# Attention's values as two block products of three factors in half the rows, with forms and buffers kept across layers

## The chip, the cores and the metric

The kernel runs on one core of a Trainium2 chip. The metric is the device time of one execution in microseconds (us). Matrix products run on TensorE (PE in the profile; its weight loads are PEld), elementwise work on VectorE (DVE) and ScalarE (ACT); GpSimd (POOL) and SyncE (SP) here only start DMAs. Each engine works through its own instructions in order.

## The reference

A decoder trunk of two layers for 256 tokens of width 2048 in float32. Layer 0 has a recurrent mixer, layer 1 dilated sliding-window attention with 16 heads of 128; each is followed by an MLP with squared ReLU (2048 to 8192 and back). What matters here is the start of layer 1:

```python
hn = rms_norm(h, norm_mix[layer])
qkv = (hn @ w_qkv).astype(F32).reshape(bsz, seq, 3, ATTN_HEADS, HEAD_DIM)
q = partial_rope(qkv[:, :, 0], positions) * (HEAD_DIM ** -0.5)
k = partial_rope(qkv[:, :, 1], positions)
v = qkv[:, :, 2]
...
out = (num / den).reshape(bsz, seq, D_MODEL).astype(h.dtype)   # softmax(q k) v, three masks merged
return out @ w_o
```

## The kernel before

**Numbers in two parts.** Float32 matrices go through TensorE as a high and a low part, and a product is high x high + high x low + low x high, three matmuls. Activations lie in `bufa` or `bufb` with both parts. Weights come from memory in units of 128 x 2048 (1 MB), and are split by `Weights.split` (lines 99 to 103): ACT copies the high part (L102), DVE subtracts to get the low part (L103). There are three buffers each for raw, high and low units. All units of the kernel stand in one list, `units`, in the order of use; `unit()` (L170) hands out the next one and starts the load and the split of the one two places further on.

**Order.** A list scheduler puts each engine's instructions in order by priority as they become ready; the loads and splits of weights have a raised priority (`stream`, offset 150), the emptying of accumulators a higher one (`urgent`, offset 400). All large matmuls are chained in program order by `mm` (L180). `turn` puts transposes into that chain, and `later`/`flush` hold back the work of `to_features` and `to_h` until a unit's matmuls are out.

**A pass of blocks() (L648).** In the MLP, two column groups of 512 are made in one pass. The 16 row blocks of the weights are in two halves. Eight plain row blocks are multiplied as usual: four units marked `n`, each for two halves of the tokens (j = 0, 1), 24 matmuls a unit. The other eight are taken in four pairs, and with two token halves and two column groups they form 2 x 2 by 2 x 2 block products, which take seven products for eight (units `a`, `t1`, `t2`, `c`, `t3`, `d`, `t4`; 12 matmuls each). The right-hand sides of four of them are sums of weight units: `s` = a + t1, then s + c (DVE, L130), `t1` with c's partner added by an accumulating DMA on POOL (L142), and for w1 a last one by such a DMA too (L148). Their left-hand sides are sums of activation blocks, the *forms*: `formx` for `bufa`, made by `to_features` (L614) with `combos` and `part_forms`, and `formh` for `bufb`. A pass makes 180 matmuls of 512 columns and 11 splits. It uses four accumulator banks: `alpha`, `delta`, `gamma` from the pool `pmm` and `beta`, named `po` or `pd`. Banks are reused within a pass, and callers give `events`, which empty a bank behind a product.

**The end of layer 0.** `mlp(0, ...)` makes four quarters of two w1 passes (`first`) and two w2 passes (`second`, adding to the residual `xres` by L751). In the last quarter each finished column group n is squared and summed for the next norm (L291), then transposed, scaled and split into `bufa` by `to_features(n, "nmix1")`, without forms (L235, L236). The groups come out in the order 1, 0, 3, 2.

**Attention.** `rstd(nx1)` makes the norm's factor `rt` (a column per token half; L295, L296, L317 to L322 on DVE); `over_tokens` transposes it into the bank `pt` (L307), ACT copies it to `rs` (L845). `tokens_group` makes four heads' values: 4 units of 24 matmuls into two banks, emptied at the end by ACT with factor `rt` (L348). `scores(u0)` projects a head's q and k (16 matmuls of 512 and 16 of 256 columns each), scales them by `rs`, turns them (`rope`, with tables made once by `rotary`, L814), and makes softmax and its transpose `pT`; `mix` multiplies by the values into `bufb`. The order is values 0, heads 0 to 3, values 1, heads 4 to 7, values 2, heads 8 to 11, the scores of heads 12 to 15, values 3, their mixes. Then `out_project` multiplies by w_o, four units of 24 matmuls for each column group, the unit of heads 12 to 15 last.

Of the kernel before, what the change touches and what calls it, by code (L numbers as in the profile page):

```python
# [41 lines left out]
def trunk_kernel(ctx, tc, x, xtok, cols, tab, masks, pos, fin, w_in, w_gate, w_out, w_qkv, w_o, w1, w2, out):  # L42
# [81 lines left out]
    def combine(u, src, i, what, i0):  # L124
        def load(name, j, home=wraw):
            held[name] = home.tile([P, 2048], F32, name="raw" if home is wraw else name)
            nc.sync.dma_start(held[name], src[j])

        def add(to, x, y):
            V.tensor_tensor(held[to], held[x], held[y], OP.add)  # L130

        if what == "a":
            load("t1", i0 + 4, pair)
            load("a", i)
            held["s"] = pair.tile([P, 2048], F32, name="s")
            add("s", "a", "t1")
        elif what in ("n", "d"):
            load(what, i)
        ahead = units[u + 1][2:3] if u + 1 < len(units) else ()
        if ahead == ("t2",):  # L140
            load("c", i0 + 5)
            nc.gpsimd.dma_start(held["t1"], src[i0 + 5], accum_op=OP.add)  # L142
            add("s", "s", "c")
        if ahead == ("t4",) and src not in T4_DMA(w1, w2):
            add("s", "s", "d")
        made[u] = Weights(held[{"t1": "s", "t2": "s", "t3": "t1", "t4": "s"}.get(what, what)])
        if what == "c" and src in T4_DMA(w1, w2):
            nc.gpsimd.dma_start(held["s"], src[i0 + 1], accum_op=OP.add)  # L148
# [175 lines left out]
    def tokens(src, i0, mov, kgs=(0, 1, 2, 3), by_k=False):  # L324
        ks = PAIRED if src is w2 else range(KB)
        ps = [pmm.tile([P, 512], F32, name="p") for _ in range(2)]
# [260 lines left out]
    def open_pairs(layer):  # L587
        pool_ = pairs.enter_context(tc.tile_pool(name=f"pair{layer}", bufs=1))
        return pool_, [pool_.tile([P, 4, 2, 512], F32R, name=n) for n in ("formx", "formh")]

# [10 lines left out]

    pair, (formx, formh) = open_pairs(0)

# [44 lines left out]
    def blocks(src, i0, n0, mov, forms, events, final):  # L648
# [20 lines left out]
        plains = [0, 0]  # L669
        for what, u in ORDERS[src is w2]:  # L670
            w = unit(src, None if u is None else i0 + 4 * n0 + u)
            if what != "n":
                times(bank[what], w, side[what])
                if what in events:
                    events[what](bank[what])
                continue
            n, g = divmod(u, 4)
            plains[n] += 1
            due = len(later)
            for j in (1, 0) if n else (0, 1):  # L680
                times(sums[n, j], w, lambda i, j=j, g=g: plain(j, 4 * g + i))
                if plains[n] == 2:
                    final(n, j, sums[n, j])
            flush(due)
# [85 lines left out]
    def mlp(layer, nrm, nxt, gname):  # L770
# [8 lines left out]
        r2 = nrm.inv_mean()  # L779
        r2n = tmp.tile([P, 2], F32, name="r2n", bufs=2)  # L780
# [26 lines left out]

    vgs = mixers.enter_context(tc.tile_pool(name="vgs1", bufs=2))
    wk = mixers.enter_context(tc.tile_pool(name="wk2", bufs=2))
    rot = mixers.enter_context(tc.tile_pool(name="rot", bufs=1))  # L810
    angles = {}
    swap = [(i + 16) % 32 for i in range(32)]

    def rotary():  # L814
        ppi = rot.tile([32, S], I32, name="ppi")
        nc.gpsimd.dma_start(ppi, bass.AP(tensor=pos.tensor, offset=pos.offset, ap=[[0, 32], [1, S]]))
        ang = rot.tile([32, S], F32, name="ang")
        cosT = rot.tile([32, S], F32, name="cosT")
        sinT = rot.tile([32, S], F32, name="sinT")
        V.tensor_copy(ang, ppi)  # L820
# [34 lines left out]
    def scores(u0):  # L855
# [20 lines left out]
        for j in range(3):  # L876
            T.transpose(pt[:, j * P:j * P + P], s[:, j * P:j * P + P], ident)
        st = wk.tile([P, 384], F32, name="pT", bufs=5)
        A.copy(st, pt)
        return st  # L880

    def mix(hd, st, vg, bank="po", bufs=1):
        vs = slice((hd % 4) * P, (hd % 4) * P + P)
        po = psc.tile([P, S], F32, name=bank, bufs=bufs)
# [3 lines left out]

    pend = []
    for g in range(4):  # L890
        if g < 3:
            vg = tokens_group(w_qkv, g * 12, rt, kgs=(0, 1, 2, 3) if g else (0, 1, 3, 2))
        if not g:
            rotary()
        for hd in range(4 * g, 4 * g + 4):
            u0 = g * 12 + (4 if g < 3 else 0) + (hd % 4) * 2
            st = scores(u0)
            if g < 3:
                mix(hd, st, vg)
            else:  # L900
                pend.append(st)
    vg = tokens_group(w_qkv, 44, rt)
    for hd, bank in zip(range(12, 16), (("po", 1), ("pd", 1), ("pl", 2), ("pl", 2))):
        mix(hd, pend[hd - 12], vg, *bank)

    mixers.close()
    pair, (formx, formh) = open_pairs(1)
    nrm = out_project(w_o, "nmlp1", (0, 1, 2, 3))
# [86 lines left out]
def _layout(a):  # L995
# [29 lines left out]
    wq = n(a["attn_w_qkv"][0])  # L1025
    q_, k_, v_ = feat(wq[:, :2048]), feat(wq[:, 2048:4096]), toks(wq[:, 4096:])
    w_qkv = []
    for g in range(4):
        if g < 3:
            w_qkv.append(v_[4 * g:4 * g + 4])  # L1030
        for h in range(4 * g, 4 * g + 4):
            w_qkv += [q_[h:h + 1], k_[h:h + 1]]
    w_qkv.append(v_[12:])
    w1 = np.concatenate([toks(n(w)[:, q * 2048:q * 2048 + 2048], PAIRED) for w in a["mlp_w1"] for q in range(4)])
# [32 lines left out]
```

## Time and profile before

| | |
|---|---|
| three runs, median (lowest to highest) | 2179.26 us (2179.17 to 2180.12) |
| the profiled execution | 2178.8 us |
| its span, first to last instruction | 2177.0 us |
| granted clock of TensorE, mean | 0.999 |
| PE busy in the span | 2148.7 us, 11044 matmuls |
| DVE, ACT busy | 1783.6 us, 1261.1 us |
| MLP of layer 0 | about 434 to 1107 us |
| attention, from the values on | about 1107 to 1403 us |

Busy times are shares of one engine's own time; engines run side by side, so they don't add up. The *chain* follows the work that ended last back through what released each step. A row of grouped instructions has the line, the engine, the operation, output and inputs, the count; then busy us, mean ns of one, and the idle time of the engine just before them with its releasers. A row of a timeline has the start, the length, and, in brackets, the idle time before it and what ended that. Each number L is a line of the kernel.

### The profile page before, as it was taken

The numbers are of one execution on the slowest core, as the hardware profiler recorded it, in microseconds if no ns is written. First come the engines' busy times: TensorE is split into PE (matmuls) and PEld (weight loads), VectorE is DVE, ScalarE is ACT, GpSimd is POOL, SyncE is SP. The second block draws the span as 40 slices with busy tenths as digits, with TensorE's granted clock in tenths as the row PEclk, the third lists the DMA queues.
The fourth block names the chain that finished last, engine by engine and source line by source line (L and its number), as shares of the span: only waits on it lengthen the run. The fifth ranks groups of instructions, "written<-read, shape, count | busy, mean of one in ns | idle before, by whom it ended". The sixth has DMA issues, their size and how long they took to land.

```text
span 2177.0 us, 27718 instructions
## 1 busy us (share of the span) xinstructions
PE 2148.7 (99%) x11044; PEld 1834.7 (84%) x11044; DVE 1783.6 (82%) x2078; ACT 1261.1 (58%) x1429; POOL 44.6 (2%) x57
## 2 busy tenths in 40 slices
PE   9999999999999999999999999999999999999997
PEld 8999998878888888888788888888888888888886
DVE  7776787779879889888877778667898898898897
ACT  7444485566466566466554544455655755755664
POOL 0000000000000000000000000000000000000000
PEclk9999999999999999999999999999999999999999
DMA  8444445577777677787655554556768777777873
GB/s 317 155 157 170 149 156 207 189 235 240 228 236 248 226 247 232 232 251 231 201 207 169 179 175 163 185 193 213 232 221 258 237 224 238 251 231 224 260 238 129
DMA packets 65857, 464.68 MB, mean 213 GB/s; under 512 B 7344, under 2 KB 8112, under 8 KB 10304
## 3 DMA queue, kind: packets, MB, share of 16 engines
q1 hardware_dynamic: 58176, 410.89, 53.2%
q0 software_dynamic: 7264, 51.42, 12.8%
q8 instruction: 87, 1.43, 0.3%
q10 hardware_dynamic: 288, 0.61, 0.1%
q14 instruction: 42, 0.34, 0.0%
HBM read 460.78 MB, written 2.10 MB: 213 GB/s over the span
## 4 chain that ended last, share of the span: by engine, by line
PE 89%; ACT 5%; DVE 3%; issue 2%; DMA 1%; SPq 0%; DVEq 0%; ACTq 0%
PE p L181 63%; PE po L181 11%; PE pd L181 10%; ACT hi L102 3%; PE pl L184 2%; DVE lo L103 1%; PE pl L476 1%; DMA raw<-in_w 0%; ACT y L720 0%; ACT formh L593 0%; ACT y L716 0%; ACT y L721 0%; PE pl L864 0%; DMA xall<-in_x 0%; PE po L885 0%
## 5 line engine op out<-in xcount | busy, mean ns | idle before, releaser
L102 ACT CAST hi<-raw 128x1024 fp32r<-128x1024 f32 (+2 forms) x486 | 689.2, 1443 | 571.4 <-PE p L181 403.1
L103 DVE TENSOR_TENSOR lo<-raw,hi 128x1024 fp32r<-128x1024 f32 (+2 forms) x486 | 822.3, 1709 | 237.7 <-ACT hi L102 219.3
L181 PE MATMUL p<-hi,bufb 128*128 128x512 f32 x1408 | 448.5, 390 | 2.2 <-DVE xall L751 2.1
L181 PE MATMUL p<-hi,bufa 128*128 128x512 f32 x1280 | 412.5, 392 | 11.3 <-ACT y L716 7.9
L181 PE MATMUL p<-bufa,hi 128*128 128x256 f32 (+1 forms) x1792 | 364.9, 317 | 0.1
L181 PEld LDWEIGHTS p<-hi,bufb 128*128 128x128 f32 x1408 | 264.3, 188 | 60.0 <-DVE xall L751 5.6
L181 PEld LDWEIGHTS p<-bufa,hi 128*128 128x128 f32 x1792 | 294.5, 190 | 18.9 <-DVE hz L418 0.3
L181 PEld LDWEIGHTS p<-hi,bufa 128*128 128x128 f32 x1280 | 240.4, 188 | 65.5 <-ACT y L716 11.3
L181 PE MATMUL p<-lo,bufb 128*128 128x512 f32 x704 | 274.1, 389 | 1.0 <-DVE lo L103 1.0
L181 PE MATMUL p<-bufa,lo 128*128 128x256 f32 x1152 | 255.5, 287 | 0.0
L181 PE MATMUL p<-lo,bufa 128*128 128x512 f32 x640 | 250.5, 391 | 1.9 <-DVE lo L103 1.9
L103 DVE TENSOR_TENSOR lo<-s,hi 128x2048 fp32r<-128x2048 f32 x96 | 219.5, 2287 | 23.2 <-ACT hi L102 21.3
L102 ACT CAST hi<-s 128x2048 fp32r<-128x2048 f32 x96 | 183.7, 1913 | 48.1 <-PE po L181 21.7
L181 PEld LDWEIGHTS p<-bufa,lo 128*128 128x128 f32 x1152 | 189.3, 191 | 2.7
L181 PEld LDWEIGHTS p<-lo,bufb 128*128 128x128 f32 x704 | 132.2, 188 | 28.3 <-DVE lo L103 1.4
L181 PEld LDWEIGHTS p<-lo,bufa 128*128 128x128 f32 x640 | 120.4, 188 | 27.1 <-DVE lo L103 3.2
L130 DVE TENSOR_TENSOR s<-s,raw 128x2048 f32<-128x2048 f32 x48 | 109.6, 2284 | 1.7 <-DMA raw<-in_w 1.7
L181 PE MATMUL pd<-hi,bufa 128*128 128x512 f32 x256 | 84.8, 392 | 0.0
L181 PE MATMUL po<-hi,bufa 128*128 128x512 f32 x256 | 84.8, 392 | 0.0
L181 PE MATMUL p<-hi,formx 128*128 128x512 f32 x256 | 84.0, 389 | 0.0
L181 PE MATMUL p<-hi,formh 128*128 128x512 f32 x256 | 84.0, 389 | 0.0
L103 DVE TENSOR_TENSOR lo<-t,hi 128x2048 fp32r<-128x2048 f32 x32 | 73.2, 2287 | 12.4 <-ACT hi L102 12.4
(281 smaller groups left out, 2765.7 us busy)
## 6 DMA issues: line engine op xcount, KB each, us to landing
raw<-in_w SPq DMA_DIRECT2D x224, 1024.0 KB, 5.1
raw<-in_w_qkv SPq DMA_DIRECT2D x48, 1024.0 KB, 4.9
raw<-in_w_in SPq DMA_DIRECT2D x46, 1024.0 KB, 4.9
t<-in_w SPq DMA_DIRECT2D x32, 1024.0 KB, 5.4
t<-in_w POOLq DMA_DIRECT2D x32, 1024.0 KB, 8.8
raw<-in_w_out SPq DMA_DIRECT2D x16, 1024.0 KB, 4.9
s<-in_w POOLq DMA_DIRECT2D x16, 1024.0 KB, 8.9
raw<-in_w_o SPq DMA_DIRECT2D x16, 1024.0 KB, 4.9
```

Of the source, the lines that this page charges most:

```text
L102: A.copy(h, w)
L103: V.tensor_tensor(l, w, h.bitcast(F32), OP.subtract)
L130: V.tensor_tensor(held[to], held[x], held[y], OP.add)
L181: chain[:] = [after(T.matmul(*args, **kw), chain)]
L184: chain[:] = [after(T.transpose(out_, in_, ident), chain)]
L476: T.matmul(pl[:, j], kq[:, js], halves(qp[:, js], c, True), start=True, stop=True)
```

## The change

- **Values.** Two calls of `values()`, each one pass of `blocks()` over 1024 columns (8 heads) of the value weights, take the place of four calls of `tokens_group`. The plain and paired row blocks are laid out as for the MLP (`PAIRED`). The pass takes the order of w2 (n7 before n6), and as for w1 its last sum is by an accumulating DMA. `beta` is the bank `pt`.
- **Scaling.** The events empty banks in the middle of the pass: ACT copies with `rt` or its negative `rtn` behind `a`, `t1` and `t2` and for one final; DVE adds to the kept values for the other four.
- **Forms.** `to_features` of column groups 0 and 1 at the end of `mlp(0)` now makes `formx` too.
- **Order.** Values of heads 0 to 7, heads 0 to 7, scores of heads 8 to 11, values of heads 8 to 15, mixes of 8 to 11, heads 12 to 15.
- **Buffers.** `t1`, `s` and `formx` move to a pool `both` that stays open over both layers. `as` has 2 buffers for 3, `pT` 4 for 5, `r2n` 1 for 2; the rotary tables share buffers with `ra` and `rb`; one value tile of twice the size takes the place of two.

```diff
     def plan2(src, i):
-        for what, u in ORDERS[src is w2]:
+        for what, u in ORDERS[src is not w1]:
...
         if layer:
-            units.extend((w_qkv, i) for i in (0, 1, 3, 2, *range(4, 48)))
+            for v, heads in ((0, 24), (32, 8)):
+                plan2(w_qkv, v)
+                units.extend((w_qkv, v + 8 + i) for i in range(heads))
...
-            load("t1", i0 + 4, pair)
+            load("t1", i0 + 4, both)
...
-            held["s"] = pair.tile([P, 2048], F32, name="s")
+            held["s"] = both.tile([P, 2048], F32, name="s")
...
-    pair, (formx, formh) = open_pairs(0)
+    both = ctx.enter_context(tc.tile_pool(name="both", bufs=1))
+    formx = both.tile([P, 4, 2, 512], F32R, name="formx")
+    pair, formh = open_pairs(0)
...
-        beta = psc.tile([P, 512], F32, name="po" if n0 else "pd", bufs=1)
+        beta = psc.tile([P, 512], F32, name="pt" if src is w_qkv else "po" if n0 else "pd", bufs=1)
...
-                    to_features(n, gname)
+                    to_features(n, gname, formx if n < 2 else None)
...
-        s = wk.tile([P, 384], F32, name="as", bufs=3)
+        s = wk.tile([P, 384], F32, name="as", bufs=2)
...
-        st = wk.tile([P, 384], F32, name="pT", bufs=5)
+        st = wk.tile([P, 384], F32, name="pT", bufs=4)
...
-    pend = []
-    for g in range(4):
-        if g < 3:
-            vg = tokens_group(w_qkv, g * 12, rt, kgs=(0, 1, 2, 3) if g else (0, 1, 3, 2))
...
+    rtn = tmp.tile([P, 2], F32, name="rtn", bufs=1)
+    V.tensor_scalar(rtn, rt, -1.0, None, op0=OP.mult)
+
+    def values(i0):
+        v = vgs.tile([P, 2, 2, 512], F32, name="vg")
+
+        def put(n, j, r=rt):
+            def event(bank):
+                with urgent():
+                    A.activation(v[:, j, n], bank, AF.Copy, scale=r[:, j:j + 1])
+            return event
+
+        def add(n, j, bank, r=rt):
+            with urgent():
+                V.scalar_tensor_tensor(v[:, j, n], bank, r[:, j:j + 1], v[:, j, n], op0=OP.mult, op1=OP.add)
+
+        blocks(w_qkv, i0, 0, bufa, formx,
+               {"a": put(0, 0), "t1": put(1, 1), "t2": put(1, 0, rtn), "t3": lambda b: add(1, 1, b, rtn)},
+               lambda n, j, b: put(n, j)(b) if (n, j) == (0, 1) else add(n, j, b))
+        return v.rearrange("p j n c -> p j (n c)")
+
+    vg = values(0)
+    rotary()
+    for hd in range(8):
+        mix(hd, scores(8 + 2 * hd), vg)
+    pend = [scores(24 + 2 * i) for i in range(4)]
+    vg = values(32)
+    for i, bank in enumerate((("po", 1), ("pd", 1), ("pl", 2), ("pl", 2))):
+        mix(8 + i, pend[i], vg, *bank)
+    for i in range(4):
+        mix(12 + i, scores(40 + 2 * i), vg)
...
-T4_DMA = lambda w1, w2: (w1,)
+T4_DMA = lambda w1, w2, w_qkv: (w1, w_qkv)
```

More of the change, by code (lines that the diff above doesn't have):

```diff
@@ L143, in combine @@
             add("s", "s", "c")
-        if ahead == ("t4",) and src not in T4_DMA(w1, w2):
+        if ahead == ("t4",) and src not in T4_DMA(w1, w2, w_qkv):
             add("s", "s", "d")
         made[u] = Weights(held[{"t1": "s", "t2": "s", "t3": "t1", "t4": "s"}.get(what, what)])
-        if what == "c" and src in T4_DMA(w1, w2):
+        if what == "c" and src in T4_DMA(w1, w2, w_qkv):
             nc.gpsimd.dma_start(held["s"], src[i0 + 1], accum_op=OP.add)
@@ L324, in tokens @@
     def tokens(src, i0, mov, kgs=(0, 1, 2, 3), by_k=False):
-        ks = PAIRED if src is w2 else range(KB)
+        ks = range(KB)
         ps = [pmm.tile([P, 512], F32, name="p") for _ in range(2)]
@@ L588, in open_pairs @@
         pool_ = pairs.enter_context(tc.tile_pool(name=f"pair{layer}", bufs=1))
-        return pool_, [pool_.tile([P, 4, 2, 512], F32R, name=n) for n in ("formx", "formh")]
+        return pool_, pool_.tile([P, 4, 2, 512], F32R, name="formh")
     def part_forms(f, k, m, at, src):
@@ L669, in blocks @@
         plains = [0, 0]
-        for what, u in ORDERS[src is w2]:
+        for what, u in ORDERS[src is not w1]:
             w = unit(src, None if u is None else i0 + 4 * n0 + u)
@@ L779, in mlp @@
         r2 = nrm.inv_mean()
-        r2n = tmp.tile([P, 2], F32, name="r2n", bufs=2)
+        r2n = tmp.tile([P, 2], F32, name="r2n", bufs=1)
         V.tensor_scalar(r2n, r2, -1.0, None, op0=OP.mult)
@@ L806, in trunk_kernel @@
     pairs.close()
-    vgs = mixers.enter_context(tc.tile_pool(name="vgs1", bufs=2))
+    vgs = mixers.enter_context(tc.tile_pool(name="vgs1", bufs=1))
     wk = mixers.enter_context(tc.tile_pool(name="wk2", bufs=2))
-    rot = mixers.enter_context(tc.tile_pool(name="rot", bufs=1))
     angles = {}
@@ L814, in rotary @@
     def rotary():
-        ppi = rot.tile([32, S], I32, name="ppi")
+        ppi = wk.tile([32, S], I32, name="ra", bufs=2)
         nc.gpsimd.dma_start(ppi, bass.AP(tensor=pos.tensor, offset=pos.offset, ap=[[0, 32], [1, S]]))
-        ang = rot.tile([32, S], F32, name="ang")
-        cosT = rot.tile([32, S], F32, name="cosT")
-        sinT = rot.tile([32, S], F32, name="sinT")
+        ang = wk.tile([32, S], F32, name="rb", bufs=2)
+        cosT = wk.tile([32, S], F32, name="cosT", bufs=1)
+        sinT = wk.tile([32, S], F32, name="sinT", bufs=1)
         V.tensor_copy(ang, ppi)
@@ L882, in mix @@
     def mix(hd, st, vg, bank="po", bufs=1):
-        vs = slice((hd % 4) * P, (hd % 4) * P + P)
+        vs = slice((hd % 8) * P, (hd % 8) * P + P)
         po = psc.tile([P, S], F32, name=bank, bufs=bufs)
@@ L887, in mix @@
         split_to(bufb[:, hd], po)
-    pend = []
-    for g in range(4):
-        if g < 3:
-            vg = tokens_group(w_qkv, g * 12, rt, kgs=(0, 1, 2, 3) if g else (0, 1, 3, 2))
[L893 to L904, printed above, removed]
+    rtn = tmp.tile([P, 2], F32, name="rtn", bufs=1)
[24 more added lines that the diff above has]
+        mix(12 + i, scores(40 + 2 * i), vg)
     mixers.close()
-    pair, (formx, formh) = open_pairs(1)
+    pair, formh = open_pairs(1)
     nrm = out_project(w_o, "nmlp1", (0, 1, 2, 3))
@@ L1025, in _layout @@
     wq = n(a["attn_w_qkv"][0])
[L1026 to L1033, printed above, removed]
+    q_, k_, v_ = feat(wq[:, :2048]), feat(wq[:, 2048:4096]), toks(wq[:, 4096:], PAIRED)
+    qk = [w[h:h + 1] for h in range(16) for w in (q_, k_)]
+    w_qkv = [v_[:8], *qk[:24], v_[8:], *qk[24:]]
     w1 = np.concatenate([toks(n(w)[:, q * 2048:q * 2048 + 2048], PAIRED) for w in a["mlp_w1"] for q in range(4)])
```

## The prediction

> **What bounds the kernel now.** I first read the page: its span, the busy times and the row of granted clocks.
>
> ```profile
> span 2177.0 us, 27718 instructions
> ...
> PE 2148.7 (99%) x11044; PEld 1834.7 (84%) x11044; DVE 1783.6 (82%) x2078; ACT 1261.1 (58%) x1429; POOL 44.6 (2%) x57
> ...
> PEclk9999999999999999999999999999999999999999
> ```
>
> The profiled execution took 2178.8 us: 1.8 us lie around the span, and it is 0.5 us under the median of 2179.26. TensorE is busy for 99% of the span at the full clock, so a matmul less is time less, and every wait of TensorE is time more. DVE, at 82%, is the engine to watch. Next come the windows, which cut the stretch around the change (columns: stretch, its length, then busy time and count of PE, PEld, DVE, ACT and POOL, granted clock, DMA share, GB/s).
>
> ```profile
> 1025.00:1065.80 40.80, 40.80 (x190) 33.97 (x189) 36.11 (x26) 23.58 (x23) 0.87 (x1) 1.00 0.70 232
> 1065.80:1106.70 40.90, 39.22 (x180) 32.00 (x179) 37.56 (x38) 23.99 (x26) 0.54 (x1) 1.00 0.55 183
> 1106.70:1129.70 23.00, 23.00 (x109) 19.07 (x108) 15.18 (x34) 13.98 (x21) 0.00 (x0) 1.00 0.54 184
> 1325.00:1377.00 52.00, 52.00 (x304) 45.83 (x303) 46.24 (x103) 24.61 (x46) 0.00 (x0) 1.00 0.48 162
> ```
>
> The first two rows are about the last two passes of blocks() in layer 0's MLP, the third is the first group of values, the fourth four heads of attention. DVE is at 89%, 92%, 66% and 89%; TensorE loses time in the second alone. Third, the chain of waits for the end of the MLP, and the timelines of PE and DVE at the same place, tell why (start, length, what):
>
> ```profile
> 1053.80 9.58 DMA raw<-in_w
> ...
> 1063.47 0.10 DVE s L130
> ...
> 1066.43 2.20 DVE lo L103
> ...
> 1072.20 3.02 PE p L181 x12
> ```
> ```profile
> 1068.68 0.50 PE L181 MATMUL p<-lo,bufb 128*128 128x512 f32 x1 [0.96 <-DVE lo L103]
> ...
> 1072.20 0.50 PE L181 MATMUL p<-hi,bufb 128*128 128x512 f32 x1 [0.72 <-DVE xall L751]
> ```
> ```profile
> 1061.90 0.47 DVE L236 SCALAR_TENSOR_TENSOR bufa<-pl,c__83,bufa 128x256 fp32r<-128x256 f32 x1
> ...
> 1063.47 2.29 DVE L130 TENSOR_TENSOR s<-s,raw 128x2048 f32<-128x2048 f32 x1 [1.09 <-DMA raw<-in_w]
> ```
>
> From 1063.5 to 1072.2 the end hangs on DVE, not on TensorE, and DVE's only free time just before is 1.09 us. Elsewhere in attention TensorE sets the pace.
>
> **The matmuls saved.** One group of values was 2 halves x 16 blocks x 3 = 96 matmuls of 512 columns. Two groups together are now 7 products x 4 x 3 = 84 and four plain units of 24, 180 for 192. Two pairs save 24.
>
> ```profile
> 1450.72 21.79 PE p L181 x96
> ```
>
> This piece of the chain is 96 such matmuls in 21.79 us, 0.227 each: 24 x 0.227 = **-5.45 us**, 0.25% of the time, and nothing else in the change can gain. The Trainium skill (TensorE: Matmul & The Clock Gate, "Wait — 56ns, not 53.3ns?") gives 215.7 ns for 512 columns; by it the term would be an estimated -5.18. The trace's row disagrees by 5%, and it is used.
>
> **What DVE gets instead.**
>
> ```profile
> L103 DVE TENSOR_TENSOR lo<-raw,hi 128x2048 fp32r<-128x2048 f32 x224 | 512.7, 2289 | 121.5 <-ACT hi L102 120.0
> ...
> L103 DVE TENSOR_TENSOR lo<-raw,hi 128x1024 fp32r<-128x1024 f32 x258 | 306.9, 1221 | 115.8 <-ACT hi L102 98.8 <-PE p L181 13.4 <-ACT as L205 2.5
> ...
> L130 DVE TENSOR_TENSOR s<-s,raw 128x2048 f32<-128x2048 f32 x48 | 109.6, 2284 | 1.7 <-DMA raw<-in_w 1.7
> ...
> L751 DVE SCALAR_TENSOR_TENSOR xall<-p,nm,xall 128x512 f32<-128x512 f32 x64 | 47.8, 746 | 13.9 <-PE p L181 13.5
> ...
> L348 ACT ACTIVATE vg<-p,nr 128x512 f32<-128x512 f32 x10 | 6.8, 689 | 11.1 <-PE p L181 8.4 <-PE po L502 2.7
> ```
>
> A pair had 8 units of two splits, 16 x 1.22 = 19.5 us of DVE. It gets 11 whole splits, 2 sums and 4 additions onto the values: 11 x 2.289 + 2 x 2.284 + 4 x 0.746 = 32.7, in 40.8 us of matmuls. ACT keeps 4 copies of 0.69 a pair. Inside a pass that is no more than the MLP's passes, which run so; the price lies where DVE is full already, which is the way into the first pair. Two loads more a pair, and two accumulating DMAs on POOL's queue, are of the MLP's kind at a DMA share of 0.54 and 0.48 in the windows of attention, below the MLP's 0.70; I cost them at nothing, and at one late landing (1.1 us, the row above) if that cover fails.
>
> **The forms at the end of the MLP.** to_features() of the first two column groups now also makes formx.
>
> ```profile
> L236 DVE SCALAR_TENSOR_TENSOR bufa<-pl,c__83,bufa 128x256 fp32r<-128x256 f32 x32 | 14.3, 476 | 0.3 <-ACT bufa L235 0.2
> ...
> L233 DVE TENSOR_TENSOR bufa<-y,bufa 128x512 fp32r<-128x512 f32 x8 | 5.5, 692 | 0.0
> ...
> L594 DVE TENSOR_TENSOR formx<-y,formx 128x512 fp32r<-128x512 f32 x8 | 5.5, 689 | 2.7 <-ACT formx L593 2.7
> ```
> ```profile
> L599 DVE TENSOR_TENSOR y<-y x8: 291/293/293, 368.7 to 1461.0; 128x128 f32<-128x128 f32 x8
> ```
>
> One call had 4 x 0.476 = 1.9 us of DVE and has 2 x (0.692 + 4 x 0.293 + 0.689) = 5.1: 3.2 more, twice. Group 1's falls at 1057 to 1062, straight ahead of the DVE-bound stretch. The 1.09 us idle hides part: 3.2 - 1.1 = **+2.1 us** (0 if it drifts behind 1072, 3.2 if the idle stays). Group 0's falls in the last pass, where the rotary tables, filler work, can be put off; I take 0, and 3.2 without that cover.
>
> **The norm in front of the first pair.** This is the largest cost, and it is a new wait. Before, a group's banks were scaled by rt and emptied only after 96 matmuls. Now t1's bank is emptied by ACT with rt, and then reused by the second half of n7, after 12 + 12 + 12 matmuls, 8.2 us into the pass.
>
> ```profile
> 1106.78 0.39 PE L181 MATMUL p<-hi,bufa 128*128 128x512 f32 x1
> ```
> ```profile
> 1107.15 0.73 DVE L751 SCALAR_TENSOR_TENSOR xall<-po,nm,xall 128x512 f32<-128x512 f32 x1
> ...
> 1111.14 0.14 DVE L295 TENSOR_REDUCE nm<-ss 128x2 f32<-128x8 f32 x1
> ...
> 1113.54 1.23 DVE L103 TENSOR_TENSOR lo<-raw,hi 128x1024 fp32r<-128x1024 f32 x1 [0.42 <-ACT hi L102]
> ...
> 1117.77 0.15 DVE L322 SCALAR_TENSOR_TENSOR nr<-rs,nr 128x2 f32<-128x2 f32 x1
> ```
> ```profile
> 1109.54 0.62 ACT L291 ACTIVATE z<-xall 128x512 bf16<-128x512 f32 x1
> ...
> 1123.05 0.37 ACT L845 COPY nr<-pt 128x256 f32<-128x256 f32 x1 [2.25 <-PE pt L307]
> ```
>
> The values begin at 1106.78, and rt is there at 1117.92, 11.1 us later: 13 tiny operations, with weight splits let in between because the stream of weights has the higher priority. Two copies of 0.69 follow, so the bank is free at 12.5: **+4.3 us** of TensorE standing still, with all later matmuls queued behind that one. From below: 13 operations at some 0.2 from 1110.3 give rt at 6.1 and the bank at 7.5, no wait. From above: three whole splits and a sum (9.2 us) ahead of the chain give 6.1. I take the row's own time, since whole splits come in for halves while to_features() of group 2 drops out behind n7.
>
> Then n6 needs group 2's features, whose transposes go out behind n7 with t2 and c (5.4 us) as cover. The MLP has the same order after an output projection:
>
> ```profile
> 1509.43 0.73 PE L181 MATMUL p<-hi,bufa 128*128 128x512 f32 x2 [1.35 <-DVE bufa L236]
> ```
>
> So **+1.4** (0 if the pause above let DVE empty its queue). The second pair meets neither. It shares only the emptying of t1's bank by ACT, which in the sixteen passes over w1 shows as
>
> ```profile
> PE p L181 <- ACT y L716: 7.9, 8, 1.0
> ```
>
> half of them, 1.0 each: **+0.5** (0 to 1.0).
>
> **What I cost at nothing.** The last head now ends attention, and its tail must be through before the output projection reaches heads 12 to 15. The tail of the first head now:
>
> ```profile
> 1146.36 3.82 PE L181 MATMUL p<-bufa,hi 128*128 128x512 f32 x16
> ...
> 1150.13 0.38 PE L863 MATMUL pl<-hz 128*128 128x128 f32 x2
> ...
> 1163.25 0.59 PE L885 MATMUL po<-pT,vg 128*128 128x256 f32 x2
> ```
>
> From the end of its key projection (1146.36, where the next starts) to its mix it took 16.9 us, drawn out by other work. The cover is three units of the output projection, 72 matmuls, 16.3 us, with DVE less busy than among heads. So 0, and up to 1.6 (with 1.0 for the mix and its split) at the first head's pace. Eight heads in a row already keep DVE at 89% and TensorE without idle time (the fourth window); if heads wait for the left-over rotary work, that costs what B costs. Fewer buffers for `as` and `pT` still cover one head and the four waiting ones.
>
> Sum: -5.45 + 2.1 + 4.3 + 1.4 + 0.5 = +2.85 us: 2181.7 for an execution like the profiled one, **2182.1** at the median.
>
> **Rivals.**
>
> A, *the wait is hidden*: the chain gets its DVE slots early and n6's features too. -5.45 + 2.1 + 0.5 = -2.85, 2176.4; with the forms hidden as well 2174.3. For it: the bounds reach it. Against: before, splits did break into the chain, for 6.8 us from reduce to rt.
>
> B, *DVE becomes the bound*.
>
> ```profile
> 1065.80:1129.70 63.90, 62.22 (x287) 51.07 (x286) 52.75 (x71) 37.97 (x47) 0.54 (x1) 1.00 0.55 184
> ```
>
> Take from this row's 52.75 us four units' splits (9.8), add the first pair (32.7) and group 0's forms (3.2): 78.8 us of DVE in 40.9 + 40.8 us, 96%. The fullest pass before had 92%. If it decides above 92%, the stretch needs 85.8 us, 4.1 more: 2186.2. Against: some rotary work can go later, and TensorE's wait for rt gives DVE time.
>
> C, *the bank of the first product*: beta is `pt`, which also holds rt's transposes. Handed out in program order, the first product waits for L845's copy. That was 16.6 us after the MLP; with TensorE idle it is rt's earliest 6.1, 0.8 for transposes and copy and half a split, some 8, and stands in place of the 4.3: 2185.8. Against: the work is put in order as it becomes ready, and the values are ready first.
>
> D, *a slower clock after the pause*: the trace's longest pauses are about 1.4 us, all at full clock, so a 4.3 us one is beyond it. If matmuls then ran at half speed for as long as the pause, 2.2 us more: 2184.3. The Trainium skill (TensorE: Matmul & The Clock Gate, "What's actually happening") has such a rule, half clock after an idle window of about 3.4 us; no row here reaches it.
>
> That the matmuls are not saved can't be: their number is fixed in the code.
>
> **How the numbers follow.** Forecast 0.40, A 0.22, B 0.18, C 0.13, D 0.07. The range of 8 in 10 goes from 2175 (A with most of the forms hidden) to 2188 (B and C with a few us on top). A difference under 0.2%, 4.4 us, is about what measuring this kernel can't tell from none. Faster (below 2174.9): two fifths of A, 0.10. Slower (above 2183.6): most of B and C, half of D, and the forecast's upper end, 0.34. Same: 0.56.
>
> **What would show it.** TensorE with 11020 matmuls for 11044 (the records can miss some); a pause of TensorE 8 us into the first pair released by ACT's copy, and rt 11 us after the MLP; a DVE wait at the end of the MLP grown by 2 us; a 1.4 us pause before n6. A first product waiting at once is C, pauses released by L103 all through the pair are B, a clock under 1.00 is D, none of them A. Wrong altogether would be a new wait in the heads or at the output projection.

## The result, and the profile after

| | before | after |
|---|---|---|
| median (lowest to highest) | 2179.26 us (2179.03 to 2180.12) | 2201.2 us (2199.6 to 2201.85) |
| the profiled execution | 2178.8 us | 2199.6 us |
| its span | 2177.0 us | 2197.5 us |
| granted clock of TensorE, mean | 0.999 | 0.994 |

The change makes the kernel 1.0% slower: 1.0099 of the time before, 95% interval 1.0085 to 1.0113. The forecast was 2182.1 and the range ended at 2188; the time lies 13 us above it. Of all executions reported in this document one fell out of line, 5586 us for the kernel before with an unused tile against 2188 to 2189 in its five others, and is left out. All line numbers below are those of the changed kernel, where most lines have moved down by two to four (L181 is L183, L236 is L238, L307 is L309, L751 is L755, L845 is L848); the two kernels made by adding to the kernel before keep its numbers. First the page after.

```profile
span 2197.5 us, 27706 instructions
...
PE 2149.2 (98%) x11020; PEld 1833.2 (83%) x11020; DVE 1813.8 (83%) x2097; ACT 1275.0 (58%) x1427; POOL 48.2 (2%) x61
...
PEclk9999999999999999999989999999999999999999
```

There are 11020 matmuls for 11044: the 24 are gone. One of the forty slices has lost clock. The windows of after, with the first two at the same place as before, and then the stretches that the timelines pointed to:

```profile
1025.00:1065.80 40.80, 40.80 (x190) 33.96 (x189) 35.55 (x25) 23.28 (x22) 0.87 (x1) 1.00 0.69 232
1065.80:1106.70 40.90, 32.44 (x146) 26.24 (x145) 37.54 (x36) 24.85 (x29) 0.87 (x1) 0.94 0.60 188
1099.00:1105.00 6.00, 0.41 (x4) 0.20 (x3) 5.58 (x9) 3.29 (x4) 0.66 (x1) 0.75 0.80 152
1105.00:1109.00 4.00, 4.00 (x12) 3.32 (x13) 2.67 (x6) 2.19 (x5) 0.00 (x0) 0.52 0.99 360
1115.50:1127.50 12.00, 0.81 (x3) 0.29 (x2) 10.47 (x33) 5.33 (x9) 0.54 (x1) 0.65 0.26 90
1127.50:1133.00 5.50, 5.27 (x13) 4.17 (x14) 0.30 (x1) 0.17 (x1) 0.00 (x0) 0.52 0.00 0
```

In the window of the MLP's last pass TensorE does 146 matmuls where it did 180 before. It stands nearly still from 1099 to 1105 and again from 1115.5 to 1127.5, and the windows behind these stretches, of 4.0 and 5.5 us, have a mean clock of 0.52. In those 12 us DVE is busy for 10.5. The timeline of PE names the waits; these are its rows that have an idle time, and one pair of matmuls at the low clock:

```profile
1069.06 0.50 PE L183 MATMUL p<-lo,bufb 128*128 128x512 f32 x1 [1.54 <-DVE lo L105]
...
1073.19 0.50 PE L183 MATMUL p<-hi,bufb 128*128 128x512 f32 x1 [1.33 <-DVE xall L755]
...
1104.91 1.09 PE L186 MATMUL pl<-tab__181,xall 128*128 128x128 f32 x4 [5.59 <-DVE bufa L238]
...
1125.85 0.69 PE L309 MATMUL pt<-tab__181,nr 128*128 128x128 f32 x2 [10.23 <-DVE nr L324]
1127.73 0.79 PE L183 MATMUL pt<-hi,bufa 128*128 128x512 f32 x1 [1.19 <-ACT nr L848]
...
1128.75 1.05 PE L183 MATMUL pt<-hi,bufa 128*128 128x512 f32 x2
```
```profile
1150.16 0.73 PE L183 MATMUL p<-hi,bufa 128*128 128x512 f32 x2 [1.45 <-DVE bufa L238]
```

The account below takes each gap as the time from one matmul's start to the next, less the usual 0.227. At the DVE-bound end of the MLP 1.70 and 1.49, before 1.12 and 0.88: +1.2. The transposes of column group 3: 5.6, then eight matmuls some 0.2 late, 1.6. Ahead of the first product of values: 10.4 + 1.4 = 11.8, then twelve matmuls 0.2 late, 2.6. n6: 1.6. A wait before the output projection's last unit: 0.5; small gaps in the second pair: 0.2. Together 25.1, less 5.45 for the matmuls: +19.7 of the span's +20.5. (The profiled execution is the fastest of five; the medians lie 21.9 us apart.)

**Why the transposes wait.** DVE and, in the last row, ACT in that stretch:

```profile
1098.18 2.28 DVE L105 TENSOR_TENSOR lo<-raw,hi 128x2048 fp32r<-128x2048 f32 x1
1100.38 0.28 DVE L599 TENSOR_TENSOR y<-y 128x128 f32<-128x128 f32 x1
1100.85 2.29 DVE L105 TENSOR_TENSOR lo<-raw,hi 128x2048 fp32r<-128x2048 f32 x1 [0.19 <-ACT hi L104]
...
1104.28 0.48 DVE L238 SCALAR_TENSOR_TENSOR bufa<-pl,c__83,bufa 128x256 fp32r<-128x256 f32 x1
1104.95 0.69 DVE L596 TENSOR_TENSOR formx<-y,formx 128x512 fp32r<-128x512 f32 x1 [0.18 <-ACT formx L595]
```
```profile
1105.67 0.84 ACT L634 ACTIVATE y<-pl,c__83 128x256 f32<-128x256 f32 x2 [0.76 <-DVE formx L596]
```

With forms, to_features copies each half of a group out of its bank `pl` into one buffer z (L632, `y21`, a single one), and then works on z. Group 0's second half can leave its bank only when z is free, that is when the first half's tiny operations (0.28 each) and its form are done; they stand in DVE's queue between splits of 2.29. So its copy comes at 1105.67, and one of the two `pl` banks is blocked until then. Group 3 has only the other bank for both its halves: its second transposes wait for L238 of its first half, at 1104.76, behind the same splits. Those transposes stand in TensorE's chain of matmuls, so all that follows waits with them.

**Why the first product waits.** It accumulates in `pt`, which was handed out in program order, behind rt's transposes and their copy. The chain of rt on DVE begins and ends so (with ACT's copy in the second fence):

```profile
1118.67 2.27 DVE L105 TENSOR_TENSOR lo<-raw,hi 128x2048 fp32r<-128x2048 f32 x1
1120.87 0.33 DVE L824 TENSOR_SCALAR rb<-rb,tab__181 32x256 f32<-32x256 f32 x1
1121.13 0.14 DVE L297 TENSOR_REDUCE nm<-ss 128x2 f32<-128x8 f32 x1
1121.24 0.28 DVE L826 TENSOR_SCALAR cosT<-rb 32x256 f32<-32x256 f32 x1
1121.45 0.15 DVE L298 TENSOR_SCALAR nm<-nm 128x2 f32<-128x2 f32 x1
...
1125.63 0.16 DVE L324 SCALAR_TENSOR_TENSOR nr<-rs,nr 128x2 f32<-128x2 f32 x1
```
```profile
1125.41 1.28 ACT L207 ACT_TABLE_LOAD   x1 [6.10 <-DVE cosT L838]
...
1127.33 0.34 ACT L848 COPY nr<-pt 128x256 f32<-128x256 f32 x1
```

DVE does not wait here; its queue is simply in this order: a split, then rt's steps one by one, most of them with a rotary operation in between, and on ACT the table for the rotary sines and the two sines ahead of the copy. rt is there at 1125.79, 10.2 us after the MLP's last matmul ended, and the copy is through at 1127.67.

### The profile page after: what moved, and what is told of

Its sections match the earlier page's. It is cut to its first block, busy times and chain, and to the rows that moved or that the text cites. A ratio compares the mean times of both kernels' runs of the same rounds, so it can differ in the third digit from the quotient of the medians.

```text
span 2197.5 us, 27706 instructions
## 1 busy us (share of the span) xinstructions
PE 2149.2 (98%) x11020; PEld 1833.2 (83%) x11020; DVE 1813.8 (83%) x2097; ACT 1275.0 (58%) x1427; POOL 48.2 (2%) x61
## 4 chain that ended last, share of the span: by engine, by line
PE 88%; ACT 6%; DVE 4%; issue 2%; DMA 1%; SPq 0%; DVEq 0%; ACTq 0%
PE p L183 61%; PE po L183 11%; PE pd L183 10%; ACT hi L104 3%; DVE lo L105 2%; PE pl L186 2%; PE pt L183 2%; PE pl L478 1%; DMA raw<-in_w 0%; ACT y L724 0%; ACT formh L595 0%; ACT y L720 0%; ACT y L725 0%; PE pl L867 0%; DVE xall L755 0%
## 5 line engine op out<-in xcount | busy, mean ns | idle before, releaser
L104 ACT CAST hi<-raw 128x2048 fp32r<-128x2048 f32 (+2 forms) x468 | 683.8, 1484 | 566.2 <-PE p L183 382.7
L105 DVE TENSOR_TENSOR lo<-raw,hi 128x2048 fp32r<-128x2048 f32 (+2 forms) x468 | 816.1, 1759 | 214.9 <-ACT hi L104 199.7
L183 PE MATMUL p<-hi,bufb 128*128 128x512 f32 x1408 | 449.3, 391 | 3.3 <-DVE xall L755 2.7
L183 PE MATMUL p<-hi,bufa 128*128 128x512 f32 x1136 | 366.5, 391 | 12.7 <-ACT y L720 7.9
L183 PE MATMUL p<-bufa,hi 128*128 128x256 f32 (+1 forms) x1792 | 365.5, 317 | 0.1
L183 PEld LDWEIGHTS p<-hi,bufb 128*128 128x128 f32 x1408 | 264.2, 188 | 61.7 <-DVE xall L755 6.2
L183 PEld LDWEIGHTS p<-bufa,hi 128*128 128x128 f32 x1792 | 294.4, 190 | 18.7 <-DVE hz L420 0.3
L183 PE MATMUL p<-lo,bufb 128*128 128x512 f32 x704 | 274.4, 390 | 1.5 <-DVE lo L105 1.5
L183 PEld LDWEIGHTS p<-hi,bufa 128*128 128x128 f32 x1136 | 213.2, 188 | 61.7 <-ACT y L720 11.3
L105 DVE TENSOR_TENSOR lo<-s,hi 128x2048 fp32r<-128x2048 f32 x102 | 233.2, 2287 | 33.6 <-ACT hi L104 31.6
L183 PE MATMUL p<-bufa,lo 128*128 128x256 f32 x1152 | 256.3, 287 | 0.0
L104 ACT CAST hi<-s 128x2048 fp32r<-128x2048 f32 x102 | 195.1, 1912 | 53.8 <-PE po L183 23.9
L183 PE MATMUL p<-lo,bufa 128*128 128x512 f32 x568 | 221.7, 390 | 1.9 <-DVE lo L105 1.9
L183 PEld LDWEIGHTS p<-bufa,lo 128*128 128x128 f32 x1152 | 189.6, 191 | 2.6
L183 PEld LDWEIGHTS p<-lo,bufb 128*128 128x128 f32 x704 | 132.2, 188 | 28.9 <-DVE lo L105 2.0
L183 PEld LDWEIGHTS p<-lo,bufa 128*128 128x128 f32 x568 | 106.7, 188 | 24.8 <-DVE lo L105 3.2
L183 PE MATMUL p<-hi,formx 128*128 128x512 f32 x288 | 95.3, 391 | 0.0
L183 PE MATMUL pd<-hi,bufa 128*128 128x512 f32 x256 | 84.8, 392 | 0.0
L183 PE MATMUL po<-hi,bufa 128*128 128x512 f32 x256 | 84.8, 392 | 0.0
L183 PE MATMUL po<-hi,bufb 128*128 128x512 f32 x256 | 84.2, 394 | 0.0
```

The lines of the kernel that those rows point to most:

```text
L104: A.copy(h, w)
L105: V.tensor_tensor(l, w, h.bitcast(F32), OP.subtract)
L183: chain[:] = [after(T.matmul(*args, **kw), chain)]
```

## The experiments

**Theory:** the loss is two new waits, for the bank `pl` behind the shared z, and for the bank `pt` behind rt, each made longer by the half clock behind it; DVE's queue sets how late rt is. **Rivals:** the order of heads or the buffers cost something of their own; DVE as a whole has become the bound; one pause merely takes the other's place, so that removing one gives little.

**Parts of the change alone.** The forms alone, made in the kernel before and used by nothing:

```diff
-                    to_features(n, gname)
+                    to_features(n, gname, formx if n < 2 else None)
```


> The kernel before with one part of the change: the forms of column groups 0 and 1 are made at the end of layer 0's MLP, and not used. Theory (the shared buffer holds a bank that transposes need): TensorE waits some 5.6 us for group 3's transposes here too, plus 1.2 of DVE and 1.6 of half clock: about 2187. Rival, as predicted blind (only DVE's 3.2 us a group count, 2.1 of them seen): 2181 to 2182.

Measured: 2187.17 us, 1.0035 of before (1.0023 to 1.0048). The transposes' wait is there without any change to the values:

```profile
1103.61 1.09 PE L184 MATMUL pl<-tab__181,xall 128*128 128x128 f32 x4 [4.61 <-DVE bufa L236]
```

So the forms cost 8 us, nearly four times the 2.1 of the forecast, and most of it is this wait and the low clock behind it.

The order and the buffers alone: the changed kernel with plain groups of values and no forms.

```diff
-        blocks(w_qkv, i0, 0, bufa, formx, ...)
+        for n in range(2):
+            ps = tokens(w_qkv, i0 + 4 * n, bufa, (0, 1, 3, 2) if not n else (0, 1, 2, 3))
+            for j in range(2):
+                put(n, j)(ps[j])
```


> The change without its passes: values in plain groups of 96 matmuls as before, no forms at the end of the MLP, but the new order of heads and values, the new buffers and the pool kept across layers. Theory (the loss lies in the waits at the end of the MLP and in front of the first pair): as before, 2179 within 1.5. Rival (order or fewer buffers cost in the heads or at the output projection): 2182 or more.

Measured: 2179.86 us, 1.0004 (0.9995 to 1.0013). They cost nothing that the times show; that rival is out.

**The waits removed one at a time.** A second z, for the second half:

```diff
-                    z = pair.tile([P, 2, 2, P], F32, name="y21")
+                    z = pair.tile([P, 2, 2, P], F32, name="y4" if half else "y21")
```


> The second half of each column group's features gets a buffer of its own (y4's, free by then) in place of sharing y21 with the first half. Theory: the transposes of group 3 waited 5.6 us for a bank that group 0's second half held while it waited for that buffer; with its own buffer the wait and the 1.6 us of half clock behind it go: about 2194. Rival (DVE is too busy, the buffer is beside the point): the transposes wait about as long, 2199 to 2201.

Measured: 2192.25 us, 1.0059 (1.0046 to 1.0072), 9 us less than the changed kernel by the medians, 6.4 by the profiled spans. The transposes no longer wait, and of the 1.70 and 1.49 us at 1069 and 1073, at the end of the MLP, a single 0.86 is left, though DVE makes the same forms. But the wait ahead of the first product has grown from 10.2 to 13.1, since TensorE now arrives there sooner:

```profile
1118.96 0.69 PE L309 MATMUL pt<-tab__181,nr 128*128 128x128 f32 x2 [13.12 <-DVE nr L324]
1120.84 0.79 PE L183 MATMUL pt<-hi,bufa 128*128 128x512 f32 x1 [1.19 <-ACT nr L848]
```

Another bank for the first product, `po`, alone and together with the second z:

```diff
-        beta = psc.tile([P, 512], F32, name="pt" if src is w_qkv else "po" if n0 else "pd", bufs=1)
+        beta = psc.tile([P, 512], F32, name="po" if n0 or src is w_qkv else "pd", bufs=1)
```


> The values' first product gets the bank po in place of pt; nothing else changes. Theory (the loss is made of single waits in front of the first pair): TensorE's 11.8 us of waiting around the transposes of rt go, and the 2.6 us of half clock behind them; the norm's factor is late all the same (10 us after the MLP), so a wait of 3 to 5 us appears at the bank of t1, 8 us into the pair. 2201.2 - 14.4 + 4 = about 2191. Rival (DVE has too much work in this stretch, whichever wait shows it): the wait only moves, 2198 to 2201.

> Both edits, the bank po and the second buffer. Theory: the waits are separate and add up, 2201.2 - 10 - 7 = about 2184, with 1 us for DVE at the end of the MLP, 4 at t1's bank and 1.6 before n6 left. Rival (DVE bound): less than the sum of the two alone, 2190 or more.

Measured: the bank alone 2195.48 us, 1.0074 (1.0061 to 1.0088), between what the theory and the rival gave; both 2190.14 us, 1.005 (1.0038 to 1.0063), 6 us over the theory and where the rival put it. The waits don't add up. PE with both:

```profile
1109.97 0.77 PE L183 MATMUL po<-hi,bufa 128*128 128x512 f32 x1 [3.73 <-DVE xall L755]
...
1126.36 0.69 PE L309 MATMUL pt<-tab__181,nr 128*128 128x128 f32 x2 [5.49 <-DVE nr L324]
1127.78 0.79 PE L183 MATMUL p<-hi,bufa 128*128 128x512 f32 x1 [0.74 <-ACT vg L901]
```

`po` was a poor choice, for the MLP's last sum still lies in it; alone, too, it cost a pause, and the matmul behind it is already at the slower clock (0.77 long):

```profile
1118.80 0.77 PE L183 MATMUL po<-hi,bufa 128*128 128x512 f32 x1 [3.11 <-DVE xall L755]
```

And with the first product under way, TensorE stops where the prediction had put the wait, at t1's bank, for 5.5 us and then 0.7 where it said 4.3. (The first of the two rows is rt's transposes, which stand just there in TensorE's queue; the second is the matmul that waits for ACT to empty t1's bank.) Both edits again, but with `pd`, which is free:

```diff
+        beta = psc.tile([P, 512], F32, name="pt" if src is w_qkv and i0 else "po" if n0 else "pd", bufs=1)
```


> As with the second buffer and another bank, but the first pair's bank is pd, which nobody holds, in place of po, which the MLP's last sum still holds. Theory (the norm's factor is set by DVE's queue, not by when TensorE starts): the 3.9 us wait in front of the first product goes, but the wait at t1's bank, 8 us later, grows by about as much; only half clock is saved, 2187 to 2189. Rival (the waits are independent): 2190.1 - 3.9 - 2.4 = 2184.

Measured: 2187.63 us, 1.0038 (1.0026 to 1.0051). Its PE rows, and two windows of it:

```profile
1113.69 0.51 PE L183 MATMUL p<-lo,bufa 128*128 128x512 f32 x1 [2.40 <-DVE lo L105]
...
1122.86 0.69 PE L309 MATMUL pt<-tab__181,nr 128*128 128x128 f32 x2 [6.33 <-DVE nr L324]
```
```profile
1124.50:1129.50 5.00, 5.00 (x12) 3.81 (x13) 0.00 (x0) 0.00 (x0) 0.00 (x0) 0.50 0.35 144
1113.60:1116.10 2.50, 2.41 (x10) 1.99 (x11) 2.50 (x5) 2.48 (x2) 0.00 (x0) 1.00 0.59 144
```

That is the theory's range: rt comes when DVE gets to it, whichever matmul it is that waits. Behind this pause of 2.40 TensorE runs on at 1.00, behind that of 6.33 at 0.50; the last section takes this up.

**Why rt is late.** Before the change most of the rotary work was done ahead of rt. The load of the positions, with which it starts, shows what moved it (before, the forms alone, and the changed kernel):

```profile
1094.47 0.54 POOL L816 DMA_DIRECT2D ppi<-in_pos  x1 [41.35 <-DVE lo L103]
```
```profile
1109.23 0.54 POOL L816 DMA_DIRECT2D ppi<-in_pos  x1 [56.23 <-DVE formx L594]
```
```profile
1115.62 0.54 POOL L819 DMA_DIRECT2D ra<-in_pos  x1 [15.96 <-DVE formx L596]
```

With forms the load is held until the last form is made from z (with a second z it starts at 1100.34); with the order and the buffers alone, without forms, it starts at 1090.36. Attention's buffers come from the memory that the MLP's pool `pair` gives up, and z lies in that pool. So the forms also push the rotary operations back, in among rt's steps. In the next kernel the rotary tables are made long before, beside layer 0's output projection; the rest is that of the last one.

```diff
+        ppi = pair.tile([32, S], I32, name="y2")
...
+        ang = pair.tile([32, S], F32, name="y4")
+        cosT = both.tile([32, S], F32, name="cosT")
+        sinT = both.tile([32, S], F32, name="sinT")
...
     vg = values(0)
-    rotary()
```


> The kernel with its own bank and the second transpose buffer (2187.63), with the rotary tables made beside layer 0's output projection and nothing else; scaling by rt stays where the change put it. Theory (rt is late because its 13 operations share DVE's queue with the rotary ones and with splits): without the rotary operations, some 3.7 us of DVE between the first and last step of rt, the wait for t1's bank falls from 6.5 to 2 to 3.5 us, the half clock behind it mostly goes, and the time is 2180 to 2183. Rival (rt is late by its own steps and the splits alone): the wait stays at 6 us and the time at 2186 to 2188.

Measured: 2182.7 us, 1.0016 (1.0007 to 1.0024), 4.9 us less. The time is as the theory had it, the wait a little longer than it said, and the half clock has not gone:

```profile
1117.98 0.43 PE L309 MATMUL pt<-tab__181,nr 128*128 128x128 f32 x2 [3.77 <-DVE nr L324]
1119.28 0.79 PE L183 MATMUL p<-hi,bufa 128*128 128x512 f32 x1 [0.87 <-ACT vg L902]
```
```profile
1118.35:1125.18 6.83, 5.96 (x16) 4.63 (x16) 0.00 (x0) 1.47 (x4) 0.00 (x0) 0.50 0.78 239
```

The rotary operations among rt's steps were thus 2.6 us of the 6.3. The wait of 2.40 inside the first product has gone as well: there DVE had stood behind the first rotary operation, which waited for the positions from memory, as this row of the kernel without the early tables shows.

```profile
1108.30 0.28 DVE L823 CAST rb<-ra 32x256 f32<-32x256 int32 x1 [2.12 <-DMA ra<-in_pos]
```

The two together, 5.0 us, are the 4.9 measured. rt now comes 12.3 us after the first matmul of the values, where it took 17.3 in the kernel without the early tables. The 3.8 us left are not taken apart by a run; in this trace two splits, 2.27 and 2.28 us, stand between rt's first and third step, more than the whole wait.

**No wait for rt at all.** The values are emptied unscaled, and ACT scales the finished ones by rt at the end of the pass. The small tile `rtn`, no longer needed, was dropped.

```diff
-    rtn = tmp.tile([P, 2], F32, name="rtn", bufs=1)
-    V.tensor_scalar(rtn, rt, -1.0, None, op0=OP.mult)
...
-        def put(n, j, r=rt):
+        def put(n, j, r=1.0):
...
+        for j in range(2):
+            A.activation(v[:, j], v[:, j], AF.Copy, scale=rt[:, j:j + 1])
```


> As the run before this one, and the values leave their banks unscaled; two ACT operations on a pair's finished values apply the norm's factor, so nothing inside the pair waits for it. Theory: the wait at t1's bank and its half clock go; left are 1 us at the end of the MLP (before: 2.2) and 1.6 before n6, so 2179.2 - 5.5 - 1.2 + 1.6 + some = 2174 to 2177, faster than before. Rival (DVE is the bound of this stretch): waits for low parts of weights take their place, 2182 or more.

And the same with the early tables:

> As the run before this one, and the rotary tables are made in layer 0, beside its output projection, in place of in front of the heads. Theory: they are filler and gain at most what they still delay, 0 to 2 us: 2173 to 2176. Rival (they crowd DVE in this stretch): 3 us or more against the run before this one.

Measured: 2189.7 us, 1.0047 (1.0033 to 1.0061), and 2183.2 us, 1.0017 (1.0008 to 1.0026): 13 and 7 us above the upper end of what was expected. Yet nothing waits for rt any more. The first keeps one wait inside the first product, 2.20 us, again behind the positions; the second has gaps of 0.6, 1.2 and 0.5 us and no more. The time had gone to every pass of the MLP in both layers, far from the change. The groups show which matmuls: here one row of that second kernel,

```profile
L183 PE MATMUL p<-hi,formx 128*128 128x512 f32 x288 | 96.9, 396 | 0.0
```

and the same group before:

```profile
L181 PE MATMUL p<-hi,formx 128*128 128x512 f32 x256 | 84.0, 389 | 0.0
```

(The 32 more are the values'.) Of the matmuls of 512 columns only those whose stationary side is a form were slower, by 5 to 6 ns each; those on `bufa` and `bufb` (391) were not. What sets the forms apart is their place: dropping `rtn` moved the pools behind it. In the built programs formx starts at byte 167744 of a partition before, after and in every kernel so far, which is a multiple of 64, and at 167712 in these two, 32 bytes off one (formh likewise). Three kernels test that: the last one with an unused tile in place of `rtn` (of the same size, and still named so), and two whose forms had been quick with one such tile added, the kernel with its own bank and the kernel before.

```diff
+    pad = tmp.tile([P, 2], F32, name="pad", bufs=1)
+    V.tensor_scalar(pad, rt, -1.0, None, op0=OP.mult)
```


> The kernel with the late scale and the early rotary tables, plus the unused 8-byte tile that the late scale had taken out of the pool ahead of the forms, so that formx and formh lie 32 bytes further on again, as in the kernel after. Theory (the matmuls whose stationary side is a form got slower by their address): in the run without the tile those 1632 matmuls took 233.4 ns from start to start for 226.7; with it they take 226.7 again, 1632 x 6.7 ns = 10.9 us less than 2183.2, so 2172.3 (2171 to 2175), faster than the kernel before by 0.2 to 0.4%. Rival (they got slower by the late scale itself, by what ACT and DVE then do): nothing moves, 2182 to 2184.

> The kernel with its own bank and the second transpose buffer (2187.63), plus one unused 8-byte tile in the pool ahead of the forms, which moves formx and formh by 32 bytes, and one DVE operation of 0.15 us. Theory (address): the matmuls with a form as stationary side go from 226.7 to 233.4 ns, 1632 x 6.7 = +10.9 us, 2196 to 2200. Rival (the late scale made them slow, not the address): 2187 to 2189.

> The kernel before, plus one unused 8-byte tile in the pool ahead of the forms, and one DVE operation of 0.15 us. Theory (address): 1536 matmuls with a form go from 226.8 to 233.4 ns, +10.1 us: 2188 to 2191, slower than the kernel before by 0.5%, though nothing is computed in another way. Rival: 2179 to 2180.

Measured: with the place restored 2175.42 us, 0.9982 of before (0.9974 to 0.9991); the shifted kernel with its own bank 2197.87, 1.0084 (1.0071 to 1.0097); the kernel before, shifted, 2188.28, 1.0041 (1.0028 to 1.0054). In the two shifted ones formx starts at 167776, again 32 bytes off. The group in the kernel before, shifted, has these rows (the matmul and its weight load, whose last column is the load engine's idle time ahead):

```profile
L181 PE MATMUL p<-hi,formx 128*128 128x512 f32 x256 | 85.6, 395 | 0.0
```
```profile
L181 PEld LDWEIGHTS p<-hi,formx 128*128 128x128 f32 x256 | 48.1, 188 | 11.4
```

With the place restored:

```profile
L183 PE MATMUL p<-hi,formx 128*128 128x512 f32 x288 | 95.4, 391 | 0.0
```

One unused tile of 8 bytes costs the kernel before 8.8 us. The theory of the place holds in both directions, and the rival is out each time. The effect came out at 7.8, 10.2 and 8.8 us where 10.9, 10.9 and 10.1 were expected: from start to start the slow matmuls take 232.7 to 233.0 ns for 226.9 on the average, some 6 ns more and not 6.7. The kernel with the place restored, 0.4 us over its expected range, is the only version here that beats the kernel before, by 0.2%. Its waits at the end of the MLP and before n6, and the window of the MLP's last pass:

```profile
1068.68 0.50 PE L183 MATMUL p<-lo,bufb 128*128 128x512 f32 x1 [0.60 <-DVE lo L105]
...
1125.93 0.73 PE L183 MATMUL p<-hi,bufa 128*128 128x512 f32 x2 [1.10 <-DVE bufa L238]
```
```profile
1065.80:1106.70 40.90, 40.30 (x187) 33.18 (x186) 40.90 (x41) 26.59 (x28) 0.86 (x1) 1.00 0.68 209
```

DVE is busy for all of that window, and TensorE loses 0.6 us. The span is 2173.3 us, 3.7 below that of before, of the 5.45 that the matmuls are worth. No run puts the second z or the early tables into the kernel before; the trace before has few waits that they could take away, 1.12 and 0.88 us at the end of the MLP, of which 0.76 is left here. So a part of the 3.7 may be theirs, not the matmuls'.

## Why the prediction was wrong

Step by step, in its own order:

- **The matmuls saved**, -5.45: right in number (11020); once the waits are gone, up to 3.7 us of the gain show.
- **DVE in the pair**, at nothing: right for the changed kernel: no split holds up the first pair behind its first product, or the second one. With the bank `pd` one did, for 2.40 us, because DVE had stood behind the positions.
- **The forms at the end of the MLP**, +2.1: this step failed. Its own term, DVE's time at 1063 to 1072, came out at 1.2, and even that went with a second z. But it counted only DVE's work, not what the work holds: "Group 0's falls in the last pass, where the rotary tables, filler work, can be put off; I take 0". There a single buffer z keeps a bank, and a transpose in TensorE's chain needs it. That is 5.6 us and 1.6 of low clock; the forms alone measured 8, the second z took 9 off. And the rotary tables were put off indeed, behind the last form and into rt's steps, which is not free: making them early took 4.9 us off.
- **The norm in front of the first pair**, +4.3: this step failed in its place and in its size. The bank `pt` was handed out in program order, so the first product waited, which was rival C. The argument against C, that the work is put in order as it becomes ready, is true of instructions; the profile shows that it wasn't so for the bank. And C's price of 8 took "rt's earliest 6.1", on the ground that TensorE is idle; TensorE's standing still did not help, for DVE's queue held a split and the rotary operations among rt's steps: 11.8. With a free bank the wait appears where the forecast had it, at t1's bank, as 6.3 and 0.7 for 4.3; with the rotary tables out of the way it is 3.8 and 0.9. The forecast read rt's 11.1 us off a trace in which most rotary work was done before.
- **n6**, +1.4: right, 1.6 by the gap.
- **The second pair**, +0.5: 0.2. **Order, buffers, last head**, 0 (up to 1.6): 0.5 in the trace, and nothing to be measured when done alone.
- **Rivals.** A is out. B is out: the kernel with the place restored keeps DVE busy for all of the MLP's last pass, and TensorE loses 0.6 us there; what cost time was the order of DVE's queue, not its load over the passes. D was right about the clock and was given 0.07: two pauses beyond 3 us, 1.6 and 2.6 us of loss. The slow stretch did not last as long as the pause: 5 us of matmuls behind one of 12.
- **The range** took the cases one at a time. C, D and the blocked bank came together, and C and D are not independent: every pause over 3 us here was followed by the low clock.

## What to carry to other kernels

When an edit gives an engine more small operations, list what they hold (banks, single buffers) and who needs that next, and price them by the largest operation that can stand ahead of each in the queue; their own time is the smaller part. Filler work that can be put off is put off into whatever comes next, so look what that is. A bank or buffer reused under an old name is ordered behind its earlier users as the program was written, so name the slowest of these before pricing the wait. And when a kernel gets slower where nothing was edited, compare the groups of one operation by operand, and look at where those operands lie.

## What the runs showed of the hardware that was not expected

- **The place of a matmul's stationary operand.** Float32 matmuls of 128x512 whose 128x128 stationary side starts 32 bytes off a multiple of 64 were 5 to 6 ns longer, group by group (390 to 396 ns on the average), and took 233 for 227 from start to start; 1536 of them made up 9 us. Two offsets were seen, 0 and 32. Whether the weight load or the matmul takes the extra time stays open: the load's own duration is 188 in both, while the idle time of the load engine ahead of this group went from 10.0 to 11.4 us. The heads' few matmuls of 256 columns, with q or the values as the stationary side, moved by the same 32 bytes and stayed at 380 and 378 ns.
- **The clock.** The length of a pause alone does not say whether the half clock follows. Four windows of the kernel with the bank `po` alone:

```profile
1115.24:1118.65 3.41, 0.45 (x2) 0.03 (x1) 3.41 (x4) 2.52 (x3) 0.54 (x1) 1.00 0.03 10
1118.65:1122.06 3.41, 3.26 (x8) 2.62 (x9) 3.41 (x10) 0.72 (x2) 0.00 (x0) 0.50 0.06 10
```
```profile
1128.89:1132.30 3.41, 0.61 (x3) 0.37 (x4) 2.05 (x5) 2.68 (x6) 0.00 (x0) 1.00 0.78 139
1132.30:1135.72 3.42, 3.42 (x9) 2.64 (x10) 0.00 (x0) 0.03 (x1) 0.00 (x0) 0.50 0.96 230
```

The first two lie around the pause of 3.11. In the third there are two pauses, of 2.05 and 0.86 us, with two short transposes between them, and yet 0.50 follows; the pause of 2.40 with the bank `pd` left the clock at 1.00. What fits all of them are steps of 3.41 us: the stretches at 0.50 around the changed part are 1 to 5 such steps long in every trace that has them (3.41 twice here; 6.83 and 13.65 in the changed kernel; 10.24 with `pd`; 17.07 with the second z alone), and the clock dropped where TensorE had been busy for 1.24 us or less of the step just ended, and not where it had been for 1.54 or more. The pause of 2.40 fell across two steps (1.55 us busy in the first). So where a pause falls among the steps counts beside its length. Near the start of some kernels a step with 1.6 to 1.9 us busy slowed it too, so the busy time is not the whole rule. At 0.50 a matmul takes 0.43 us for 0.227, and the matmuls behind a pause stayed there for 3.4 to 6 us. The Trainium skill (TensorE: Matmul & The Clock Gate, "What's actually happening") states half the clock after an idle window of about 3.4 us, and full clock again after a busy one. The trace agrees with the half and with the length; but the window need not be idle throughout, 1.24 us of work in it did not keep the clock up.
